# The running sum of a row gather moves into PSUM, and its rows are issued at a closer pace

## The chip, the cores and the metric

The kernel runs on one core of a Trainium2 chip, as one launch. The metric is the device time of that launch in microseconds (us). The core's engines, as the profile names them: PE (matrix products, with PEld for its weight loads), DVE (vector operations), ACT (activations and copies), POOL (some vector operations, and it issues the gathering DMAs), SP (issues the other DMAs). SBUF is the on-chip memory that all of them work in; PSUM is the small memory that PE writes its products to, which this kernel uses as eight banks of 128 x 512 f32.

## The reference

Two small networks in a row, everything in f32, on 256 tokens of width 1024. The first has two layers, each a feed-forward block, a mixer (retention in the first, latent attention in the second) and another feed-forward block. Its result `x` goes into the second network, which has two layers again; each is a mixer and a mixture of 16384 experts per layer, of which every token uses 128. Beside `x` the second network carries 256 context tokens through its first layer; the context does not depend on `x`.

```python
def second_block(x, c, ctx, c_ctx, ...):
    hl, hc = x, ctx
    for i in range(2):
        ml = (silu(c) @ mod_w[i] + mod_b[i])        # six modulation rows each
        mc = (silu(c_ctx) @ mod_w[i] + mod_b[i])
        xl, xc = modulate(rmsnorm(hl), ml), modulate(rmsnorm(hc), mc)
        yl, yc = _even_mixer(xl, xc, ...) if i == 0 else _odd_mixer(xl, xc, ...)
        hl = hl + ml[2] * yl
        hl = hl + ml[5] * _peer_ffn(modulate(rmsnorm(hl), ml), ...)
        if i == 0:                                    # the context ends here
            hc = hc + mc[2] * yc
            hc = hc + mc[5] * _peer_ffn(modulate(rmsnorm(hc), mc), ...)
    return rmsnorm(hl, final_g)

def _peer_ffn(xt, w_q, keys, u, v):                   # per token
    q = (xt @ w_q).reshape(n, 8, 2, 128)
    sv, si = top_k(einsum('nhpd,hpkd->nhpk', q, keys), 16)
    cand = sv[:, :, 0, :, None] + sv[:, :, 1, None, :]
    cs, ci = top_k(cand.reshape(n, 8, -1), 16)        # 8 heads x 16 experts
    eidx = ...                                        # expert = 128 * si0 + si1
    w = softmax(cs) * gelu(einsum('nd,nhkd->nhk', xt, u[eidx]))
    return einsum('nhk,nhkd->nd', w, v[eidx])
```

The experts of the latent tokens are computed densely (all 16384, with the unused gates at zero); those of the context tokens are gathered, row by row.

## The kernel before

**Two streams.** `run_streams` steps two generators. The main stream is the chain from `x` to the output: memory, the feed-forward block ffn00, retention, ffn01, ffn10, latent attention, ffn11, the even mixer, `peer_dense` of layer 0, the odd mixer, `peer_dense` of layer 1. The side stream has the context's work: its even mixer, its route (`ctx_route`: eight groups of scores, and `route_pick`, which ends in the expert numbers `eidx`), and then `gather`. Each `yield` gives a cost, and the stream whose clock (`tm`, `ts`) is behind goes on; the clock also sets the priority by which a list scheduler then orders every engine's instructions. Each engine executes its list strictly in order, so a row that waits holds all rows behind it on its engine.

**Gather.** For each of two tiles of 128 tokens, 128 rows of the table u0 and then 128 of v0: 512 rows, each an indirect DMA issued by POOL (128 x 1024 f32, 512 KB) into one of `GR` = 6 buffers, and one DVE instruction. For u0 that is a dot product with the tokens `pxm` (`dot`, L306), for v0 a multiply-add into the running sum `py` (L1628). Tokens, rows and sum all lie in SBUF. After every second row the stream yields `s.gcost`, 6.5 all along.

**Modulation beside it.** Every third step of the gather also takes a step of `mod1`: seven modulation slots, each of eight 512 KB weight blocks (loaded by POOL's queue) times a narrow `cT`, 32 products and four for the bias, summed in one PSUM bank (L888).

**PSUM banks.** Three kinds: "acc" has four banks (the accumulators of a feed-forward block or of the downs), "w" two (the products of the main stream's weights), "c" two (the context's products, `mod1`, and the second step of several attention and routing stages).

**Products.** Most f32 weights are split into two parts: ACT casts (`wh`, L248), DVE or POOL subtracts (`wl`, L255), and PE multiplies three times (L357 to L359). A feed-forward block is 22 units; one unit is 48 rows of PE for gate and up and 12 for down, with a product `sg` and a subtraction `hlo` on DVE between them. `peer_dense` has 64 ups and 64 downs. The first `AR` ups run before the downs, the others one per down; each down has a cast `Wh` on ACT (L259) and `Wl` on DVE (L260). Of the ups, the first `NU` are multiplied at full f32 (L404, without a split). Between the route and the downs, `spread_gates` builds the gate matrix.

## Time and profile before

| | |
|---|---|
| time, median of 3 runs | 3910.0 us (3907.83 to 3913.4) |
| the profiled execution: its own time | 3902.65 us |
| its span, first to last instruction | 3899.7 us |
| mean granted PE clock | 0.932 of full speed |
| PE busy | 3444.3 us, 88% |
| DVE busy | 2800.3 us, 72% |
| ACT, POOL busy | 1564.8 us, 1507.2 us |
| data moved by DMA | 938.13 MB, mean 241 GB/s |
| gather's rows on DVE (L306, L1628) | 341.8 and 410.0 us |

Stages of the main stream in the trace, from the span's start: ffn00 to about 565 us, retention to 767, ffn01 to about 1000, ffn10 to about 1213, latent attention to 1330, ffn11 to 1590, even mixer to 1845, `peer_dense` 0 to 2838 (its downs from 2158 to 2827), odd mixer to 3020, `peer_dense` 1 to 3888. The gather's first DMA is issued at 567.4 us and its last at 2807.1 us. The busy shares are means over stages: PE is the busiest engine of the whole and of most stages, yet DVE has almost no free time in some.

### The profile page before, as it was taken

To read this page: it belongs to the slowest core of one execution; us is meant where nothing else is said; L and a number is where in the kernel's file an instruction comes from. 1 tells how busy PE (TensorE), PEld (TensorE's weight loads), DVE (VectorE), ACT (ScalarE), POOL (GpSimd) and SP (SyncE) were. 2 spreads that over 40 slices of the span, in tenths; PEclk is the share of its full clock that TensorE was granted. 3 is DMA by queue.
4 is the path that set the end of the run, shared out by engine and by line. 5 is a ranking of instruction groups with operands and counts; after the bars stand their busy time and mean duration, and the time that the engine had idled before them with its cause. 6 is when DMAs were issued, how large, how long until landed. Compare 5 with 4: busy or idle time off the path is not lost.

```text
span 3899.7 us, 55086 instructions
## 1 busy us (share of the span) xinstructions
PE 3444.3 (88%) x20560; PEld 2939.3 (75%) x20560; DVE 2800.3 (72%) x5086; ACT 1564.8 (40%) x2432; POOL 1507.2 (39%) x1014
## 2 busy tenths in 40 slices
PE   5998868799897889788798899999878999999998
PEld 3776867588686678666687788887665889889987
DVE  4456798867777677877798788889976629754444
ACT  3454433334343443433123344444345215444444
POOL 3423325455554245431335477777710000122221
PEclk9999989899898899867899899999989999999999
DMA  7547459878787478753779999999951447876664
GB/s 271 155 146 236 159 163 381 278 278 279 265 294 274 151 252 306 273 175 97 252 272 361 319 324 331 332 333 321 341 154 34 141 156 253 274 238 216 195 192 151
DMA packets 316508, 938.13 MB, mean 241 GB/s; under 512 B 34512, under 2 KB 99504, under 8 KB 312144
## 3 DMA queue, kind: packets, MB, share of 16 engines
q1 hardware_dynamic: 216912, 578.77, 44.4%
q0 software_dynamic: 99328, 355.85, 25.8%
q8 instruction: 161, 2.64, 0.3%
q14 instruction: 107, 0.88, 0.1%
HBM read 894.82 MB, written 39.68 MB: 240 GB/s over the span
## 4 chain that ended last, share of the span: by engine, by line
PE 34%; issue 10%; DVE 9%; POOL 7%; DMA 5%; ACT 2%; POOLq 0%; SPq 0%; DVEq 0%; ACTq 0%
PE ps L357 8%; PE ps L358 8%; PE ps L359 7%; PE ps L404 6%; POOL pg L1600 4%; POOL wl L255 3%; PE ps L313 1%; DMA raw<-in_ffn 1%; DVE py L1628 1%; DVE wl L255 1%; DVE pg L306 1%; PE ps L1661 1%; DMA raw<-in_ut 1%; PE ps L1112 1%; ACT wh L248 1%
## 5 line engine op out<-in xcount | busy, mean ns | idle before, releaser
L248 ACT CAST wh<-raw 128x1024 fp32r<-128x1024 f32 (+3 forms) x925 | 915.6, 992 | 1028.6 <-PE ps L359 674.5
L255 POOL TENSOR_TENSOR wl<-raw,wh 128x1024 fp32r<-128x1024 f32 (+2 forms) x274 | 641.5, 2342 | 1342.4 <-ACT wh L248 1239.2
L255 DVE TENSOR_TENSOR wl<-raw,wh 128x1024 fp32r<-128x1024 f32 (+3 forms) x651 | 799.7, 1233 | 404.5 <-ACT wh L248 403.7
L357 PE MATMUL ps<-xh,wl 128*128 128x256 f32 x2992 | 868.0, 290 | 69.2 <-POOL wl L255 38.9
L358 PE MATMUL ps<-xl,wh 128*128 128x256 f32 x2992 | 857.2, 287 | 0.0
L359 PE MATMUL ps<-xh,wh 128*128 128x256 f32 x2992 | 856.2, 286 | 0.0
L357 PEld LDWEIGHTS ps<-xh,wl 128*128 128x128 f32 x2992 | 582.9, 195 | 101.6 <-POOL wl L255 51.0
L358 PEld LDWEIGHTS ps<-xl,wh 128*128 128x128 f32 x2992 | 583.3, 195 | 5.3 <-issue 0.7
L359 PEld LDWEIGHTS ps<-xh,wh 128*128 128x128 f32 x2992 | 582.4, 195 | 3.5 <-issue 3.2
L1600 POOL DMA_INDIRECT pg<-in_v,eidx x256 | 371.7, 1452 | 395.2 <-DVE py L1628 200.6
L1600 POOL DMA_INDIRECT pg<-in_u,eidx x256 | 370.3, 1447 | 376.4 <-DVE pg L306 277.3
L358 PE MATMUL ps<-wl,Wh 128*128 128x512 f32 x1024 | 408.0, 398 | 26.0 <-POOL wl L255 14.8
L357 PE MATMUL ps<-wh,Wl 128*128 128x512 f32 x1024 | 403.1, 394 | 12.3 <-DVE Wl L260 12.3
L1628 DVE SCALAR_TENSOR_TENSOR py<-pg,pA,py 128x1024 f32<-128x1024 f32 x254 | 410.0, 1614 | 3.4 <-DMA pg<-in_v,eidx 0.3
L359 PE MATMUL ps<-wh,Wh 128*128 128x512 f32 x1024 | 401.6, 392 | 0.0
L404 PE MATMUL ps<-xf,raw 128*128 128x256 f32 x1696 | 382.8, 386 | 2.3 <-ACT xf L332 2.3
L404 PEld LDWEIGHTS ps<-xf,raw 128*128 128x128 f32 x1696 | 325.3, 194 | 47.2 <-ACT xf L332 3.1
L306 DVE SCALAR_TENSOR_TENSOR pg<-pg,pxm 128x1024 f32<-128x1024 f32 x256 | 341.8, 1360 | 11.6 <-DMA pg<-in_u,eidx 11.4
L358 PE MATMUL ps<-wl,xh 128*128 128x512 f32 (+4 forms) x656 | 254.1, 387 | 13.7 <-POOL wl L255 8.4
L358 PEld LDWEIGHTS ps<-wl,Wh 128*128 128x128 f32 x1024 | 194.2, 190 | 81.3 <-POOL wl L255 22.7
L357 PE MATMUL ps<-wh,xl 128*128 128x512 f32 (+4 forms) x656 | 248.3, 386 | 6.6 <-ACT wh L248 2.8
L359 PE MATMUL ps<-wh,xh 128*128 128x512 f32 (+4 forms) x656 | 248.1, 379 | 0.0
(481 smaller groups left out, 4768.7 us busy)
## 6 DMA issues: line engine op xcount, KB each, us to landing
raw<-in_ffn SPq DMA_DIRECT2D x264, 512.0 KB, 5.1
raw<-in_ut SPq DMA_DIRECT2D x256, 512.0 KB, 5.3
raw<-in_v SPq DMA_DIRECT2D x256, 512.0 KB, 4.9
raw<-in_modw POOLq DMA_DIRECT2D x96, 512.0 KB, 6.5
Gd<-Gst SPq DMA_DIRECT2D x32, 1024.0 KB, 7.2
Gq<-Gd SPq DMA_DIRECT2D x30, 1024.0 KB, 8.4
raw<-in_wq SPq DMA_DIRECT2D x32, 512.0 KB, 3.9
raw<-in_evin POOLq DMA_DIRECT2D x24, 512.0 KB, 4.0
```

What stands on the lines that cost most here:

```text
L248: nc.scalar.copy(hi, src)
L255: eng.tensor_tensor(lo, src, hi.bitcast(F32), op=OP.subtract)
L306: return s.nc.vector.scalar_tensor_tensor(a, a, 1.0, b, op0=OP.mult, op1=OP.mult, accum_out=out)
L313: s.nc.tensor.transpose(dst, src, s.ident[:src.shape[0], :src.shape[0]])
L357: mm(out, a[1], b[0], start=start, stop=False)
L358: mm(out, a[0], b[1], start=False, stop=False)
L359: mm(out, a[0], b[0], start=False, stop=stop)
L404: s.nc.tensor.matmul(out, src[:, k * 128:(k + 1) * 128], xf[:, k], start=(k == 0), stop=(k == 7))
L1112: nc.tensor.matmul(po[:, :128], pt[:, k], srcs[k // 2][key][:, k % 2, h * 128:(h + 1) * 128], start=(k == 0), stop=(k == m - 1))
L1600: nc.gpsimd.indirect_dma_start(out=got[i], out_offset=None, in_=d[tab], in_offset=bass.IndirectOffsetOnAxis(ap=eidx[t][:, k:k + 1], axis=0))
L1628: s.pin(nc.vector.scalar_tensor_tensor(y, gt, wk, y, op0=OP.mult, op1=OP.add))
L1661: nc.tensor.matmul(pb[:, t * 128:(t + 1) * 128], M[:, k, :, t0 + t], OJ[:, (t0 + t) // 2, :, t % 2], start=(k == 0), stop=(k == 1))
```

## The change

The sum `py` and the tokens `pxm` move to PSUM: `gather` opens a PSUM pool of its own, `psg`, of two banks, loads the tokens to SBUF (`pxs`) and lets ACT copy them over. A dot or a multiply-add then has one operand in SBUF (the gathered row) and the other in PSUM. The two "c" banks exist no more as such while the gather runs; they are opened for the context's work up to the end of its route (`pss`) and again in the odd mixer (`pso`). What used "c" in between uses other kinds: the attention and mixer stages "w", the route and the gates of `peer_dense` "acc" (its accumulators are taken later), `mod1` "w", that is the two banks of the main stream's weights. So that `mod1` does not hold such a bank over several steps, it ends a partial sum after every two weight blocks, and DVE collects the four of a slot in SBUF (`modo`).

`GC`, the cost of a gather step, is 5.3 instead of 6.5 until the main stream comes to `peer_dense` 0, and 6.5 from there. In layer 0 `AR`, `NU` go from 19 to 18. The condition `cT` is made once, at the start, and not once for each call of `modulation`.

```diff
     def bank(s, kind="w"):
-        return s.psp.tile([128, 512], F32, tag=kind, name=s.nm("ps"), bufs={"acc": 4, "w": 2, "c": 2}[kind])
+        return (s.psc if kind == "c" else s.psp).tile([128, 512], F32, tag=kind, name=s.nm("ps"), bufs=4 if kind == "acc" else 2)
...
-                pb = s.bank("c")
+                if kind == "c":
+                    pb, o = s.bank(kind), bias
+                else:
+                    o = pl.tile([128, 256], F32, name=s.nm("modo"), tag="modo")
                 for k in range(8):
+                    if kind != "c" and k % 2 == 0:
+                        pb = s.bank(kind)
                     fetch(units.index((l, a, k)) + MP)
                     raw = raws.pop((l, a, k))
                     for ps, ns in qs:
-                        nc.tensor.matmul(pb[ps, :256], c[:, k], raw(ns.start, ns.stop), start=(k == 0), stop=False)
-                    if k % 2:
+                        nc.tensor.matmul(pb[ps, :256], c[:, k], raw(ns.start, ns.stop), start=(k % (8 if kind == "c" else 2) == 0),
+                                         stop=(kind != "c" and k in (1, 3, 5)))
+                    if kind != "c" and k == 1:
+                        nc.vector.tensor_copy(o, pb[:, :256])
+                    elif kind != "c" and k in (3, 5):
+                        nc.vector.tensor_tensor(o, o, pb[:, :256], op=OP.add)
...
-        with s.pool("pgg", side) as op:
+        with s.pool("pgg", side) as op, s.psum("psg") as pg:
...
-                xm = op.tile([128, D], F32, tag="pxy", name=s.nm("pxm"))
-                s.dq(xm, xmd[t])
+                xs = op.tile([128, D], F32, tag="pxy", name=s.nm("pxs"))
+                s.dq(xs, xmd[t])
+                xm = pg.tile([128, D], F32, tag="pxy", name=s.nm("pxm"))
+                nc.scalar.copy(xm, xs)
...
-                y = op.tile([128, D], F32, tag="pxy", name=s.nm("py"))
+                y = pg.tile([128, D], F32, tag="pxy", name=s.nm("py"))
...
-        A0N, AR = ((8, 19), (18, 34))[l]
+        A0N, AR = ((8, 18), (18, 34))[l]
...
-            accs = s.acc4()
...
-                yield from s.route_scores(rp, rp, xT, l, "w", "c", xf=xf)
+                yield from s.route_scores(rp, rp, xT, l, "w", "acc", xf=xf)
...
-            yield from s.modulation("right", [(0, 5)] + [(1, a) for a in (1, 0, 2, 4, 3, 5)], MC[2])
+            yield from s.modulation("right", [(0, 5)] + [(1, a) for a in (1, 0, 2, 4, 3, 5)], MC[2], "w")
...
-GC = (6.5, 6.5)
+GC = (5.3, 6.5)
```

**Order, place one.** PE of the kernel before at the end of the context's scores (`keys` times `pq`, L1460); `ps_1311` to `ps_1313` are accumulators of ffn00, whose 16 units were begun by then.

```order
L357 MATMUL ps_1311<-wh_4920,hlo_4756 128x512
L358 MATMUL ps_1311<-wl_4922,hh_4755 128x512
L359 MATMUL ps_1311<-wh_4920,hh_4755 128x512
L357 MATMUL ps_1312<-wh_4920,hlo_4756 128x512
L1460 MATMUL ps_3858<-keys_3789,pq_3856 128x128 x4
L358 MATMUL ps_1312<-wl_4922,hh_4755 128x512
L359 MATMUL ps_1312<-wh_4920,hh_4755 128x512
L357 MATMUL ps_1313<-wh_4920,hlo_4756 128x512
```

ffn00 goes on at once, and the first rows of `mod1` (L888) stand some 410 rows later, in retention. The same place on PE in the changed kernel, where `xh_2885` belongs to the context and `xh_1241` to ffn00:

```order
L362 MATMUL ps_3787<-xl_2886,wh_3836 128x256
L363 MATMUL ps_3787<-xh_2885,wh_3836 128x256
L1487 MATMUL ps_3854<-keys_3785,pq_3852 128x128 x4
L903 MATMUL ps_4574<-raw_4372,cT_288 32x256
L361 MATMUL ps_4592<-xh_1241,wl_4595 128x256
L362 MATMUL ps_4592<-xl_1242,wh_4593 128x256
L363 MATMUL ps_4592<-xh_1241,wh_4593 128x256
```

The first row of `mod1` (L903) now stands directly behind the scores and ahead of ten of ffn00's 22 units of gate and up and eleven of down. Its weights `raw_4372` are issued by POOL, whose list has ten gather DMAs ahead of them (the first and the last two, then the weights):

```order
L1627 DMA pg_4167<-in_u,eidx_2877 128x1024
L1627 DMA pg_4360<-in_u,eidx_2877 128x1024
L1627 DMA pg_4363<-in_u,eidx_2877 128x1024
L197 DMA raw_4372<-in_modw 128x1024
L197 DMA raw_4374<-in_modw 128x1024
```

These need `eidx`, the end of the pick. In the kernel before, the same weights stood behind ten gather DMAs too, but no row of ffn00 stood behind them on PE.

**Place two.** DVE of the kernel before at the end of the pick (`eq`, `cpart`, `eidx`), with rows of ffn00 (`wl`, `sg`, `hlo`) between the pick's, 26 in all:

```order
L1519 TENSOR_TENSOR eq_4138<-io_4112,rd_4134 128x2048
L255 TENSOR_TENSOR wl_5549<-raw_5537,wh_5547 128x1024
L1522 TENSOR_TENSOR eq_4138<-eq_4138,SIf_4136 128x2048
L514 TENSOR_TENSOR sg_5512<-sg_5512,ps_5439 128x256
L1523 TENSOR_REDUCE cpart_4133<-eq_4138 128x128
L260 TENSOR_TENSOR hlo_5516<-sg_5512,hh_5515 128x256
L255 TENSOR_TENSOR wl_5553<-raw_5539,wh_5551 128x1024
```

In the changed kernel the pick has no row of ffn00 in it, twelve dots follow, and the first product of ffn00, `sg_4665`, stands behind the copy of `mod1`'s first partial sum:

```order
L1591 CAST eidx_2878<-cpart_4110 128x128
L310 SCALAR_TENSOR_TENSOR pg_4167,pA_4179<-pg_4167,pxm_4177 128x1024
...
L310 SCALAR_TENSOR_TENSOR pg_4467,pA_4179<-pg_4467,pxm_4177 128x1024
L906 COPY modo_4573<-ps_4574 128x256
L518 TENSOR_TENSOR sg_4665<-sg_4665,ps_4592 128x256
L259 TENSOR_TENSOR wl_4741<-raw_4562,wh_4739 128x1024
```

**Place three.** DVE of the kernel before among the last six downs of `peer_dense` 0 (`Wl` is one per down, `py` is one per gathered row):

```order
L260 TENSOR_TENSOR Wl_25186<-A_24068,Wh_25185 128x512
L255 TENSOR_TENSOR wl_25191<-raw_25180,wh_25189 128x1024
L1628 SCALAR_TENSOR_TENSOR py_21457<-pg_25073,pA_16722,py_21457 128x1024
L1628 SCALAR_TENSOR_TENSOR py_21457<-pg_25076,pA_16722,py_21457 128x1024
L1628 SCALAR_TENSOR_TENSOR py_21457<-pg_25122,pA_16722,py_21457 128x1024
L260 TENSOR_TENSOR Wl_25229<-A_24180,Wh_25228 128x512
```

In the changed kernel the last rows of the sum and its end (`bc`, `px`) stand at the 45th of the 64 downs, and the remaining downs have no gathered row beside them:

```order
L264 TENSOR_TENSOR Wl_24383<-A_22433,Wh_24382 128x512
L1657 SCALAR_TENSOR_TENSOR py_19704<-pg_24147,pA_14995,py_19704 128x1024
L259 TENSOR_TENSOR wl_24278<-raw_24265,wh_24276 128x1024
L1657 SCALAR_TENSOR_TENSOR py_19704<-pg_24150,pA_14995,py_19704 128x1024
L1743 TENSOR_TENSOR A_24255<-A_24255,Gq_25021 128x512
L1663 TENSOR_TENSOR bc_24367<-bc_24367,py_19704 128x1024
```

Counted on DVE's lists, the gathered rows done when the main stream reaches a point are, before and now: end of ffn00 0 and 36, of retention 60 and 70, of ffn01 108 and 126, of ffn10 156 and 179, of latent attention 168 and 202, of ffn11 222 and 267, start of `peer_dense` 0 256 and 314, its first down 330 and 386, its 46th down 459 and 512. PE's rows of `mod1` in retention go from 117 to 16; 29, 60 and about 60 rows now stand inside ffn00, ffn01 and ffn10, where before they stood between the stages.

## Rows read from the trace of the kernel before

**Rows 1.** Windows: length, busy us (instructions) PE, PEld, DVE, ACT, POOL; clock, DMA, GB/s.
```profile
565.00:767.00 202.00, 154.50 (x894) 126.55 (x895) 167.36 (x374) 70.48 (x123) 99.00 (x101) 0.84 0.90 327
2159.00:2712.00 553.00, 522.32 (x3213) 462.51 (x3214) 483.87 (x409) 234.38 (x272) 394.69 (x209) 0.99 0.94 329
2712.00:2827.00 115.00, 96.65 (x389) 72.06 (x387) 114.40 (x82) 41.91 (x48) 88.74 (x52) 0.99 0.93 341
```

**Rows 2.** ACT's timeline: casts Wh, one per down, in both expert layers.
```profile
2158.64 1.14 ACT L259 CAST Wh<-A 128x512 fp32r<-128x512 f32 x2 [3.68 <-DMA Gd<-Gst]
2712.88 0.62 ACT L259 CAST Wh<-A 128x512 fp32r<-128x512 f32 x1 [1.66 <-PE ps L359]
2827.06 0.62 ACT L259 CAST Wh<-A 128x512 fp32r<-128x512 f32 x1 [1.66 <-PE ps L359]
3451.81 0.61 ACT L259 CAST Wh<-A 128x512 fp32r<-128x512 f32 x1
3463.03 0.61 ACT L259 CAST Wh<-A 128x512 fp32r<-128x512 f32 x1
3708.92 0.62 ACT L259 CAST Wh<-A 128x512 fp32r<-128x512 f32 x1 [1.67 <-PE ps L359]
3714.36 0.62 ACT L259 CAST Wh<-A 128x512 fp32r<-128x512 f32 x1 [1.67 <-PE ps L359]
```

**Rows 3.** ACT's timeline: first and last of the route's eight score copies.
```profile
419.57 0.59 ACT L1463 COPY psc<-ps 128x512 f32<-128x512 f32 x1
491.68 0.59 ACT L1463 COPY psc<-ps 128x512 f32<-128x512 f32 x1 [1.30 <-PE ps L1460]
```

**Rows 4.** DVE's timeline there: feed-forward result, first dot, twelfth dot.
```profile
563.62 1.89 DVE L469 SCALAR_TENSOR_TENSOR xn<-ps,bc 128x512 f32<-128x512 f32 x3
576.77 1.23 DVE L306 SCALAR_TENSOR_TENSOR pg<-pg,pxm 128x1024 f32<-128x1024 f32 x1 [4.23 <-DMA pg<-in_u,eidx]
597.90 1.22 DVE L306 SCALAR_TENSOR_TENSOR pg<-pg,pxm 128x1024 f32<-128x1024 f32 x1
```

**Rows 5.** DVE's groups from 498 to 568 us, the feed-forward's: busy us, mean ns, idle.
```profile
L255 DVE TENSOR_TENSOR wl<-raw,wh 128x1024 fp32r<-128x1024 f32 x14 | 16.9, 1214 | 0.9 <-ACT wh L248 0.9
L260 DVE TENSOR_TENSOR hlo<-sg,hh 128x256 fp32r<-128x256 f32 x6 | 3.3, 555 | 0.0
```

**Rows 6.** POOL's timeline at the start of the gather: start, length, instruction.
```profile
567.36 1.02 POOL L1600 DMA_INDIRECT pg<-in_u,eidx  x1 [0.55 <-DVE eidx L1564]
584.74 1.12 POOL L197 DMA_DIRECT2D raw<-in_modw  x2
```

**Rows 7.** Transfers of the page: issues, KB each, us to landing.
```profile
raw<-in_modw POOLq DMA_DIRECT2D x96, 512.0 KB, 6.5
```

**Rows 8.** ACT's timeline in one feed-forward stage: casts 1 and 18.
```profile
1041.64 0.41 ACT L259 CAST hh<-sg 128x256 fp32r<-128x256 f32 x1
...
1200.53 0.41 ACT L259 CAST hh<-sg 128x256 fp32r<-128x256 f32 x1 [3.27 <-DVE sg L514]
```

**Rows 9.** PE's waits: 760 to 1000, 965 to 1225, 1220 to 1340 us; total, times, longest.
```profile
PE ps L888 <- DMA raw<-in_modw: 8.8, 2, 6.9
PE ps L888 <- DMA raw<-in_modw: 10.5, 4, 6.6
PE ps L888 <- DMA raw<-in_modw: 14.1, 6, 5.8
```

**Rows 10.** The costliest groups of the page: busy us, mean ns, idle before.
```profile
L1628 DVE SCALAR_TENSOR_TENSOR py<-pg,pA,py 128x1024 f32<-128x1024 f32 x254 | 410.0, 1614 | 3.4 <-DMA pg<-in_v,eidx 0.3
L306 DVE SCALAR_TENSOR_TENSOR pg<-pg,pxm 128x1024 f32<-128x1024 f32 x256 | 341.8, 1360 | 11.6 <-DMA pg<-in_u,eidx 11.4
```

**Rows 11.** The running sum's instructions: ns min/median/max, first and last start.
```profile
L1628 DVE SCALAR_TENSOR_TENSOR py<-pg,pA,py x254: 1249/1282/3840, 1124.1 to 2819.9; 128x1024 f32<-128x1024 f32 x127
```

**Rows 12.** DVE groups by form: one input in PSUM, then both in SBUF.
```profile
L912 DVE TENSOR_TENSOR fo<-ps,bc 128x512 f32<-128x512 f32 x4 | 2.7, 692 | 4.8 <-PE ps L359 4.6
L913 DVE TENSOR_TENSOR x<-x,fo 128x512 f32<-128x512 f32 x4 | 2.6, 684 | 0.0
```

More of the change, by code (lines that the diff above doesn't have):

```diff
@@ L849, in mla, with condition, modulation @@
             yield from s.out_proj(x, mix, d["wo1"], g3)
-    def modulation(s, side, slots, cost):
+    def condition(s, pl):
+        nc = s.nc
+        c = pl.tile([128, 8, 32], F32, name=s.nm("cT"))
+        nc.vector.memset(c, 0.0)
+        cr = pl.tile([128, 8, 2], F32, name=s.nm("cR"))
+        s.dq(cr, s.d["cvecT"])
+        nc.scalar.activation(c[:, :, 0:2], cr, AF.Silu)
+        one = pl.tile([128, 32], F32, name=s.nm("one"))
+        nc.vector.memset(one, 1.0)
+        s.cond = (c, one)
+    def modulation(s, side, slots, cost, kind="c"):
         nc, d = s.nc, s.d
@@ L892, in modulation @@
                     nc.tensor.matmul(pb[ps, :256], one[ps.start:ps.start + 1], bias[ps.start:ps.start + 1], start=False, stop=True)
[L893 removed]
+                if kind != "c":
+                    nc.vector.tensor_tensor(o, o, pb[:, :256], op=OP.add)
+                    pb = o
                 if a in (1, 4):
[L895 removed]
+                    pg = s.bank(kind)
                     for ps, ns in qs:
@@ L1633, in gather @@
                 s.dq(x, hc[t])
-                nc.vector.tensor_tensor(y, y, g, op=OP.mult)
-                nc.vector.tensor_tensor(x, x, y, op=OP.add)
+                nc.vector.tensor_tensor(g, g, y, op=OP.mult)
+                nc.vector.tensor_tensor(x, x, g, op=OP.add)
                 s.dq(s.hc1[t], x)
@@ L1837, in side @@
         yield from wait("start")
+        pc = ExitStack()
+        s.psc = pc.enter_context(s.psum("pss"))
         with s.pool("pgo", R) as po:
+            s.condition(po)
             with s.pool("sraw", R) as rp:
```

30 lines of the change are left out of this document (16 added, 14 removed).

## The prediction

> **What bounds the kernel now.** I read the windows first, to see which engine fills which stage. In the downs of `peer_dense` 0 PE is busy for 522 of 553 us, DVE for 484, and DMA stands at 0.94; in the last sixteen downs DVE is full (114.4 of 115 us) and PE is not (96.7); in retention neither PE (154.5 of 202) nor DVE (167) is full, and DMA is at 0.90 [rows 1]. So the gather costs time in three ways: it fills DVE at the end of the downs, it fills DMA and DVE in retention, and its modulation makes PE wait between the stages.
>
> The casts of `Wh` say how much it costs in the downs. In `peer_dense` 1, which has no gather beside it, a down with an up takes 3463.03 - 3451.81 = 11.22 us, and a down alone 5.44 us. In `peer_dense` 0 the 47 downs to 2712.88 took 554.2 us; 45 with an up and 2 without would be 45 x 11.22 + 2 x 5.44 = 515.8, so 38 us are lost. The last 16 took 114.2 us and would be 87.0, so 27 us are lost [rows 2].
>
> Then I read the end of ffn00, since the order moves most there. The eight score copies of the context's route run from 419.57 to 491.68, 10.3 us a group [rows 3]; the first gather DMA is issued at 567.36 and the first modulation weights 17.4 us later [rows 6]. ffn00 is over at 563.6, before the first dot [rows 4].
>
> **The change part by part.** All terms are made against the profiled execution's own 3902.65 us; the median of the runs shown is 3910.0, 7.35 us more, and that is added at the end. What one measurement of this kernel can tell from no change is about 0.2%, 8 us.
>
> *The hole in ffn00, +76.* In the new order PE comes to `mod1`'s first product with ten units of gate and up and eleven of down still to do, and that product waits for weights that POOL issues behind ten gather DMAs, which wait for the end of the pick. I date it so. The scores begin two units earlier, since PE has done 12 units and not 14 by then: at 9.35 us a unit (casts 1 and 18 of a feed-forward stage lie 158.9 us apart [rows 8]) that would be 19 us, but the context's own chain ahead of the scores is only partly PE's, so I take 14, thus 406. The groups have no ffn00 unit between them now; of 10.3 us a group, two units in seven groups were 2 x 9.35 / 7 = 2.7, which leaves 7.6; I take 8.5, since DVE's top-k of a group may then set the pace: the last copy at 466. From the last copy to the first gather DMA it was 75.7 us, of which ffn00's subtractions on DVE took 16.9 + 3.3 [rows 5] and its products a little more; without them 54: the first gather at 520. The weights are issued 17.4 us later and land in 6.5 [rows 6, 7]: PE goes on at 544. Ten and a quarter units at 9.35 are 96 us: ffn00 ends at 640 in place of 563.6. The bounds: +55 if the remaining units run at PE's bare pace and the scores begin 19 us earlier, +95 if groups stay at 10 us and `sg`, which stands behind twelve dots and the copy of `modo`, is late as well: the twelfth dot ended 31.7 us after the first gather DMA (597.90 + 1.22 against 567.36 [rows 4, 6]), 8 us behind the weights.
>
> *Retention, -38.* It has 34 gathered rows in place of 60, and 16 products of `mod1` in place of 117. 26 rows are 26 x (1.36 + 0.08) = 37 us of DVE [rows 10] in a stage where DVE is busy for 167 of 202 us, and 26 x 512 KB, 13.6 MB, which at 327 GB/s is 42 us of a nearly full DMA [rows 1]. PE's 154.5 us set the floor: at most -48. At least -10, if the chain of norms and decays sets it.
>
> *Waits between stages, -27.* PE waits for modulation weights by 8.8, 10.5 and 14.1 us around the ends of ffn01, ffn10 and in latent attention [rows 9], 33.4 in all. The products that wait there stand inside the feed-forward blocks now, fetched two ahead. Most of it goes; between -10 and -35.
>
> *Inside the stages, +12.* Counted on DVE's lists, ffn01, ffn10, latent attention, ffn11 and the even mixer take 8, 5, 11, 11 and 13 rows more than before; at 1.44 us these 48 rows are 69 us of DVE, which is busy for about three quarters of those stages, and `mod1` takes one of the main stream's two "w" banks at times. A quarter of it on the path is 17; less a little for rows that no longer stall, 12. Bounds -15 (the sum in PSUM relieves these stages too) and +30.
>
> *The last downs, -27.* The gather is done at the 45th of 64 downs, so the last 16 run at 5.44 us. The cover that DVE took away is given back whole; -20 if DMA, at 0.93 there [rows 1], holds them up by itself.
>
> *The other downs, -24.* The number of rows beside them is nearly the same, 126 for 129. But a multiply-add costs 1614 ns in the mean, a dot 1360 [rows 10], while the fastest multiply-add is 1249, the median 1282 and the slowest 3840 [rows 11]: the mean is made by stalls of a few, next to POOL's own subtractions. With one operand in PSUM I expect most of these to go. What that is worth on the path is bounded by the 38 us that these downs lose [rows 2]; nothing, if DMA at 0.94 bounds them. I take some two thirds, since PE's waits there are for subtractions and not for weights.
>
> [...]
>
> *What an operand in PSUM costs, 0.* The trace has one pair of the same instruction: 692 ns with an input from PSUM, 684 with both in SBUF [rows 12]. That is 8 ns, 4 us of DVE over 512 rows; nothing in before writes PSUM from DVE.
>
> [...]
>
> *The rest, -4.* The pick of `peer_dense` 0 has two rows less, and the odd mixer has the context's result earlier: -6. One up goes from the gates to the downs, where it takes three products for two slower ones, two casts and two subtractions: +2, hidden in what DVE gains. `condition` at the start costs nothing: it runs beside the memory stage's loads. The 23 additions and 7 copies of `modo`, 128 x 256, are 30 x 0.4 us over 1500 us, off the path; the two copies to PSUM are ACT's, which is busy for two fifths.
>
> Sum: 76 - 38 - 27 + 12 - 27 - 24 - 4 = -32. 3902.65 - 32 + 7.35 = **3878**.
>
> **The rivals.**
>
> *The hole is not given back (slower).* ffn00 ends 76 us late, and retention is bound by its own chain of norms, transposes and decays, so that fewer rows there win 10; the waits for weights only move into the feed-forward blocks: -10 and +25; the last downs -20, the others -5, the rest 0. Together +56, or 3966; where only some of these terms fall short the time lies between 3918 and 3966. It decides where retention and the stages up to `peer_dense` 0 give back less than 30 us of the 76. For it speaks that PE stands still for some 75 us in a place where nothing was lost before; against it that retention has both DVE and DMA loaded with just the rows that it loses.
>
> *The stalls were worth more (faster still).* With the sum in PSUM, POOL's subtractions are no longer held up anywhere, the feed-forward blocks gain 15 and the other downs their whole 38; retention -48, waits -35, last downs -31: 76 - 48 - 35 - 15 - 31 - 38 - 4 = -95, or 3815. It needs the feed-forward pace of 9.35 us to fall towards PE's own. The high DMA share of the downs speaks against it.
>
> *Nothing in sum (3902 to 3918).* The hole takes all that the downs, retention and the waits give; for this it is enough that two of the three give half.
>
> *The hole is not there.* If the weights of `mod1` were there before PE comes to them, the +76 would fall away, and the time be near 3800. POOL's list excludes it: ten gather DMAs, all behind `eidx`, stand ahead.
>
> **How the numbers follow.** My forecast, 3825 to 3902, 0.47; the larger gain, below 3825, 0.09; nothing in sum, 0.13; slower, 0.30; the hole absent, 0.01, counted with the larger gain. The time is that of the first. The range leaves out about one in ten below and one in ten above, the upper part of the slower case: 3825 to 3948. The forecast's own range is 3845 to 3902. Faster by over 0.2%: 0.57; within: 0.13; slower: 0.30.
>
> **What the new profile would show.** PE waiting for `raw<-in_modw` once for 60 to 85 us shortly before 550, and ffn00 ending near 640. Retention from there in about 165 us in place of 202. No wait over 5 us for modulation weights after it. `Wh` casts 5.4 us apart in the last sixteen downs, and a mean of the multiply-adds near 1.3 us. I am wrong if ffn00 ends before 600 (another order of arrival at the weights than I read), if retention still takes over 185 us, or if the multiply-add's mean stays above 1.5 us: then two SBUF operands were not what made some of them slow.

## The result and the profile after

The changed kernel takes 3941.22 us (median of 6 runs, 3916.19 to 3945.97) where the kernel before takes 3911.24. The ratio on record, which is not simply the quotient of the two medians, is 1.0069, with a 95% interval of 1.0046 to 1.0091. Ten more runs on another occasion gave 3933.41 us against 3905.66, 1.0067 (1.005 to 1.0084). By the medians it is slower by 28 to 30 us. Its profiled execution is the fastest of the first six, 3916.19 us; the span of this profile is 14.7 us longer than before's.

The page's head, span and busy time of each engine:

```profile
span 3914.4 us, 55149 instructions
PE 3416.5 (87%) x20576; PEld 2944.5 (75%) x20576; DVE 2688.3 (69%) x5107; ACT 1567.4 (40%) x2434; POOL 1362.2 (35%) x1011
```

DVE has 112 us less to do than before, and the kernel is slower all the same. The place where this begins is in PE's timeline, with the wait before a row and its releaser in brackets:

```profile
547.92 1.06 PE L903 MATMUL ps<-raw,cT 128*32 128x256 f32 x2 [65.91 <-DMA raw<-in_modw]
```

PE stands still for 65.9 us in ffn00, for the first weights of `mod1`, and the rows of ffn00 that stand behind this product on its list stand still with it: the next (L361) starts at 548.91 us, though its operands were there, since DVE and POOL make no `wl` between 475.5 and 555.5 us. The same stretch by windows (columns as in [rows 1]):

```profile
480.00:500.00 20.00, 1.33 (x10) 0.97 (x8) 17.40 (x150) 2.45 (x3) 0.00 (x0) 0.65 0.00 0
500.00:520.00 20.00, 0.00 (x0) 0.00 (x0) 19.73 (x59) 1.33 (x2) 0.00 (x0) 0.50 0.07 27
520.00:550.00 30.00, 2.08 (x7) 1.27 (x8) 21.33 (x32) 0.00 (x0) 15.38 (x17) 0.50 0.63 235
550.00:560.00 10.00, 9.46 (x69) 8.67 (x69) 4.19 (x7) 4.05 (x5) 4.34 (x4) 0.79 0.58 224
```

From 500 to 520 us PE has no product at all, DVE works on the context's route and its pick alone, and the granted clock falls from 0.65 to 0.50. When PE goes on, from 550 to 560, the mean is 0.79. POOL's timeline shows why the weights are late. Its list holds the gather's DMAs ahead of them:

```profile
529.15 1.02 POOL L1627 DMA_INDIRECT pg<-in_u,eidx  x1 [54.37 <-DVE eidx L1591]
541.36 1.16 POOL L197 DMA_DIRECT2D raw<-in_modw  x2
```

And DVE's timeline shows the dating of the prediction step by step, from the second `eidx` to the end of ffn00:

```profile
528.91 0.23 DVE L1591 CAST eidx<-cpart 128x128 int32<-128x128 f32 x1
533.61 1.22 DVE L310 SCALAR_TENSOR_TENSOR pg<-pg,pxm 128x1024 f32<-128x1024 f32 x1 [4.48 <-DMA pg<-in_u,eidx]
558.27 0.42 DVE L906 COPY modo<-ps 128x256 f32<-128x256 f32 x1 [5.23 <-PE ps L903]
558.61 0.41 DVE L518 TENSOR_TENSOR sg<-sg,ps 128x256 f32<-128x256 f32 x1
649.25 2.48 DVE L473 SCALAR_TENSOR_TENSOR xn<-ps,bc 128x512 f32<-128x512 f32 x4 [5.51 <-PE ps L363]
```

The first gather DMA is at 529.2 (forecast 520), PE goes on at 547.9 (544), ffn00 ends at 649.25 (640), 85.6 us behind before's 563.62 [rows 4].

What PE waits for between the stages, in the three places that answer to [rows 9]:

```profile
PE ps L317 <- DVE sm L289: 13.8, 1, 13.8
PE ps L317 <- DVE sm L289: 10.6, 1, 10.6
PE ps L317 <- DVE sm L289: 24.6, 1, 24.6
```

No wait there is for modulation weights any more, and yet PE waits 13.8, 10.6 and 24.6 us, for the chain of norms (`sm`), 49.0 in all. In the windows of [rows 9] the kernel before waited for `sm` as well, 1.2, 6.0 and 4.6 us; with the 33.4 for the weights that is 45.2.

The instructions on the gathered rows, minimum, median and maximum in ns, to be read against [rows 11]:

```profile
L310 DVE SCALAR_TENSOR_TENSOR pg<-pg,pxm x256: 1160/1212/1225, 533.6 to 2187.0; 128x1024 f32<-128x1024 f32 x128
L1657 DVE SCALAR_TENSOR_TENSOR py<-pg,pA,py x254: 1270/1281/1291, 1117.5 to 2712.4; 128x1024 f32<-128x1024 f32 x127
L1655 DVE TENSOR_SCALAR py<-pg,pA x2: 1277/1282/1287, 1116.1 to 2201.4; 128x1024 f32<-128x1024 f32 x2
```

The slowest multiply-add takes 1291 ns where it took 3840. Of the downs of `peer_dense` 0, ACT's timeline has these casts of `Wh`, the first and the last two of 64:

```profile
2220.78 1.14 ACT L263 CAST Wh<-A 128x512 fp32r<-128x512 f32 x2 [4.72 <-DMA Gd<-Gst]
2838.34 0.62 ACT L263 CAST Wh<-A 128x512 fp32r<-128x512 f32 x1 [1.67 <-PE ps L363]
2843.78 0.62 ACT L263 CAST Wh<-A 128x512 fp32r<-128x512 f32 x1 [1.66 <-PE ps L363]
```

and these are the windows of retention, of the downs, and of the last downs:

```profile
649.00:832.00 183.00, 148.55 (x822) 126.09 (x822) 149.53 (x338) 71.74 (x124) 58.68 (x59) 0.82 0.70 243
2225.00:2740.00 515.00, 499.79 (x3143) 452.56 (x3142) 412.42 (x337) 227.93 (x263) 314.62 (x190) 0.99 0.95 335
2740.00:2850.00 110.00, 110.00 (x531) 92.98 (x530) 43.77 (x44) 53.02 (x61) 38.35 (x16) 1.00 0.61 192
```

Retention has DMA at 0.70 where it was 0.90 [rows 1], and PE at 148.5 of 183 us. The last downs run at 5.44 us, with PE full and DVE at two fifths. The 64 downs take 623.0 us from the first cast to the last; they took 668.4 [rows 2]. With the 48th cast, at 2751.96 us, the first 47 take 531.2 us (554.2 before) and the last 16 91.8 (114.2). These 91.8 are more than 16 times 5.44, since `AR` is 18 now and one of the 16 still has an up.

The stages of the two kernels and of seven experiments (their numbers in brackets), in us, each from one profiled execution and measured from the first row of one stage's result on DVE to that of the next (`xn<-ps`, `pa<-ps` and `IJ<-ps` in the timelines); the first column is the time from the start of the span. "pick" is the route of `peer_dense` 0 up to `IJ`, "dense 0" the rest of it. A profile can lie off its kernel's median: the changed kernel's lies 17 to 25 us below, that of experiment 1 lies 15 above.

| kernel | ffn00 ends | retention | ffn01 | ffn10 | latent att. | ffn11 | even | pick | dense 0 | odd |
|---|---|---|---|---|---|---|---|---|---|---|
| before | 563.6 | 203.5 | 232.4 | 239.3 | 127.2 | 222.5 | 254.1 | 164.2 | 828.2 | 165.0 |
| changed | 649.2 | 182.6 | 241.6 | 231.8 | 129.4 | 225.0 | 254.1 | 159.5 | 778.1 | 164.6 |
| mod1 held (1) | 565.1 | 223.4 | 243.1 | 235.7 | 123.7 | 227.9 | 249.5 | 159.7 | 783.5 | 169.6 |
| pace undone (2) | 648.3 | 178.3 | 241.1 | 239.8 | 113.2 | 219.0 | 237.6 | 163.2 | 790.3 | 167.3 |
| sum in SBUF (3) | 656.5 | 187.8 | 251.6 | 240.6 | 130.1 | 234.1 | 260.6 | 159.9 | 797.8 | 164.7 |
| before, pace alone (4) | 561.9 | 216.4 | 233.2 | 234.6 | 120.8 | 234.6 | 261.3 | 162.0 | 802.0 | 164.0 |
| held, pace undone (5) | 562.6 | 201.7 | 234.9 | 234.0 | 118.0 | 226.3 | 247.4 | 163.2 | 785.3 | 165.3 |
| held, SBUF, 6.5 (10) | 568.1 | 204.2 | 242.0 | 234.7 | 118.5 | 236.6 | 245.7 | 165.9 | 829.3 | 169.8 |
| held, SBUF, 5.3 (11) | 557.7 | 217.6 | 248.6 | 246.6 | 125.3 | 241.6 | 260.7 | 159.3 | 795.4 | 164.3 |

### The profile page after: what moved, and what is told of

It is laid out like the page before. It is cut to its first block, busy times and chain, and to the rows that moved or that the text cites. A ratio compares the mean times of both kernels' runs of the same rounds, so it can differ in the third digit from the quotient of the medians.

```text
span 3914.4 us, 55149 instructions
## 1 busy us (share of the span) xinstructions
PE 3416.5 (87%) x20576; PEld 2944.5 (75%) x20576; DVE 2688.3 (69%) x5107; ACT 1567.4 (40%) x2434; POOL 1362.2 (35%) x1011
## 4 chain that ended last, share of the span: by engine, by line
PE 56%; DVE 17%; issue 11%; DMA 8%; POOL 5%; ACT 3%; SPq 0%; POOLq 0%; DVEq 0%; ACTq 0%
PE ps L361 14%; PE ps L362 14%; PE ps L363 14%; PE ps L408 6%; POOL pg L1627 2%; DMA raw<-in_ffn 2%; POOL wl L259 2%; PE ps L317 2%; DVE pg L310 2%; DVE wl L259 2%; DMA raw<-in_modw 1%; DVE py L1657 1%; ACT wh L252 1%; DMA pg<-in_u,eidx 1%; DMA Gq<-Gd 1%
## 5 line engine op out<-in xcount | busy, mean ns | idle before, releaser
L259 DVE TENSOR_TENSOR wl<-raw,wh 128x1024 fp32r<-128x1024 f32 (+3 forms) x653 | 777.1, 1193 | 536.9 <-ACT wh L252 534.0
L259 POOL TENSOR_TENSOR wl<-raw,wh 128x1024 fp32r<-128x1024 f32 (+2 forms) x274 | 621.3, 2269 | 1435.3 <-ACT wh L252 1263.3
L361 PE MATMUL ps<-xh,wl 128*128 128x256 f32 x3008 | 873.6, 290 | 64.1 <-DVE wl L259 33.4
L363 PE MATMUL ps<-xh,wh 128*128 128x256 f32 x3008 | 864.6, 287 | 0.0
L361 PEld LDWEIGHTS ps<-xh,wl 128*128 128x128 f32 x3008 | 589.5, 196 | 93.7 <-DVE wl L259 39.3
L363 PEld LDWEIGHTS ps<-xh,wh 128*128 128x128 f32 x3008 | 589.4, 196 | 3.5 <-issue 3.1
L1627 POOL DMA_INDIRECT pg<-in_u,eidx x256 | 297.9, 1164 | 542.0 <-DVE pg L310 325.4
L1627 POOL DMA_INDIRECT pg<-in_v,eidx x256 | 320.6, 1252 | 306.3 <-DVE py L1657 198.3
L361 PE MATMUL ps<-wh,Wl 128*128 128x512 f32 x1024 | 401.2, 392 | 7.9 <-DVE Wl L264 7.9
L363 PE MATMUL ps<-wh,Wh 128*128 128x512 f32 x1024 | 399.6, 390 | 0.0
L408 PE MATMUL ps<-xf,raw 128*128 128x256 f32 x1664 | 368.9, 382 | 2.3 <-ACT xf L336 2.3
L408 PEld LDWEIGHTS ps<-xf,raw 128*128 128x128 f32 x1664 | 317.1, 192 | 45.8 <-ACT xf L336 3.1
L1657 DVE SCALAR_TENSOR_TENSOR py<-pg,pA,py 128x1024 f32<-128x1024 f32 x254 | 325.6, 1282 | 3.1
L310 DVE SCALAR_TENSOR_TENSOR pg<-pg,pxm 128x1024 f32<-128x1024 f32 x256 | 305.2, 1212 | 22.8 <-DMA pg<-in_u,eidx 22.1
L362 PE MATMUL ps<-wl,xh 128*128 128x512 f32 (+4 forms) x656 | 254.3, 388 | 15.5 <-POOL wl L259 10.6
L361 PE MATMUL ps<-wh,xl 128*128 128x512 f32 (+4 forms) x656 | 248.3, 386 | 6.8 <-ACT wh L252 4.6
L363 PE MATMUL ps<-wh,xh 128*128 128x512 f32 (+4 forms) x656 | 249.4, 380 | 0.0
L361 PEld LDWEIGHTS ps<-wh,Wl 128*128 128x128 f32 x1024 | 193.5, 189 | 46.6 <-DVE Wl L264 7.3
```

What stands on the lines that cost most here:

```text
L259: eng.tensor_tensor(lo, src, hi.bitcast(F32), op=OP.subtract)
L310: return s.nc.vector.scalar_tensor_tensor(a, a, 1.0, b, op0=OP.mult, op1=OP.mult, accum_out=out)
L361: mm(out, a[1], b[0], start=start, stop=False)
L362: mm(out, a[0], b[1], start=False, stop=False)
L363: mm(out, a[0], b[0], start=False, stop=stop)
L408: s.nc.tensor.matmul(out, src[:, k * 128:(k + 1) * 128], xf[:, k], start=(k == 0), stop=(k == 7))
```

## The experiments

**1. mod1 held back until ffn00 is done.**

```diff
+        if not s.modgo:
+            return 0
         s.nalong += 1
         if s.nalong % ME:
             return 0
...
                     yield from s.ffn(x, d[f"ffn{l}0"], gain(6 * l + 0), gain(6 * l + 1))
+                    s.modgo = True
```

> The changed kernel, with the steps of mod1 held back until the main stream has left ffn00; all else as changed. Theory 1 (the loss is the 65.9 us for which PE waits for the first modulation weights in ffn00): that wait is gone, ffn00 ends within 10 us of before's 563.6 us, peer_dense 0 keeps its gain of some 50 us, and the time is 3845 to 3875 us, some 1 to 1.7% faster than before. Rival (the hole only moves work: what stood still is done later by a stage that has to wait instead): retention takes over 215 us in place of 203 and the time stays within 10 us of the kernel before, 3900 to 3920 us.

Measured: 3870.16 us (3866.5 to 3885.63), 0.9906 of before (0.9886 to 0.9925). PE's waits from 440 to 600 us, total, times, longest:

```profile
PE ps L317 <- DVE xn L342: 21.2, 2, 19.3
PE ps L361 <- DVE wl L259: 4.9, 5, 2.5
```

The wait for the weights is gone, ffn00 ends at 565.1, `peer_dense` 0 keeps its gain. The 21.2 us are the norm at retention's start, which before shows too (23.0). Retention does pay some of it back, 223.4 us, but the time says that most of the hole was a loss: 63 to 71 us by the two medians of the changed kernel. The two profiles differ by 30.6 us only, since one is the slowest of its four runs and the other the fastest of its six. The same pair at the old pace, experiments 2 and 5, gives 66 us by medians and 58.5 by profiles. That the shared banks put `mod1`'s product at this place is read from the lists: experiments 2 and 3 rule out the pace and the operand, but no run gave `mod1` a bank of its own in the changed kernel.

**2. The pace undone.**

```diff
-GC = (5.3, 6.5)
+GC = (6.5, 6.5)
```

> The changed kernel with a gather step's cost at 6.5 as before, so that only the pace is undone. Theory 1: the hole in ffn00 stays (a wait of 55 to 70 us), since it comes from the shared bank and not from the pace; the gathered rows reach into the last downs again, which loses some 10 to 25 us there: 3945 to 3965 us. Rival (the closer pace makes the hole and burdens the stages before the experts): the wait is below 30 us and the time at or below 3910 us.

Measured: 3897.52 us (3890.61 to 3910.62), 0.9976 of before (0.9958 to 0.9994). Neither expectation, though the rival's time came true: the hole is untouched,

```profile
PE ps L903 <- DMA raw<-in_modw: 66.5, 1, 66.5
```

so it does not come from the pace, as theory 1 has it; but the kernel is 36 to 44 us faster than the changed one, where theory 1 had it slower. The stages say where: latent attention 113.2 for 129.4, the even mixer 237.6 for 254.1, ffn11 219.0 for 225.0, retention 178.3 for 182.6, and in return 12 us lost in dense 0, 8 in ffn10 and 4 in the pick. The windows of latent attention and the even mixer, first of the changed kernel, then of this one:

```profile
1307.00:1437.00 130.00, 88.10 (x457) 75.14 (x458) 91.55 (x232) 57.56 (x145) 41.45 (x34) 0.80 0.50 170
1660.00:1914.00 254.00, 207.70 (x826) 158.44 (x825) 201.61 (x573) 102.52 (x207) 76.64 (x60) 0.73 0.54 190
```

```profile
1307.00:1422.00 115.00, 86.39 (x484) 72.41 (x485) 75.98 (x221) 56.93 (x142) 32.47 (x29) 0.85 0.50 179
1640.00:1877.00 237.00, 194.84 (x825) 148.68 (x824) 193.99 (x510) 100.41 (x206) 56.03 (x46) 0.75 0.49 172
```

In the changed kernel DVE has 15.6 us more to do in latent attention (14 more gathered rows in the trace) and the stage takes 16.2 longer; in the even mixer it is 13 rows and 16.5 us, of which DVE's busy time has 7.6. The wait for the chain of norms (`sm`) at the start of latent attention is 24.6 us there, above, and here

```profile
PE ps L317 <- DVE sm L289: 15.2, 1, 15.2
```

So in latent attention rows that come between the steps of such a chain seem to be paid for whole. In ffn01 and ffn10 the changed kernel has ten rows more and these cost nothing. That this holds of mixers and feed-forward blocks in general is not shown: between before and experiment 4, where the pace alone differs, latent attention has eight rows more and is 6.4 us shorter, and ffn11 has nine more and is 12 longer. What the profiles do bear is the sum. From the end of ffn00 to the end of the even mixer the changed kernel takes 35.7 us longer than this one, for 57 rows more.

**3. The sum in SBUF, all else as changed.** The pool `psg` and the copy to PSUM are taken out; `pxm` and `py` come from the SBUF pool, as before.

> The changed kernel with the tokens and the running sum in SBUF again, banks and pace as changed. If the operand in PSUM is what takes the stalls away: the multiply-add's mean goes from 1282 ns back over 1500, the downs of peer_dense 0 lose 15 to 35 us, and the time is 3950 to 3980 us. Rival (the downs gained by the rows that moved forward, not by the operand): the mean goes back, yet peer_dense 0 stays within 8 us, and the time is that of the changed kernel within 10 us.

Measured: 3988.4 us (3983.59 to 3990.33), 1.0213 of before (1.0195 to 1.0232). The stalls are back:

```profile
L310 DVE SCALAR_TENSOR_TENSOR pg<-pg,pxm x256: 1161/1218/4344, 536.4 to 2229.5; 128x1024 f32<-128x1024 f32 x128
L1655 DVE SCALAR_TENSOR_TENSOR py<-pg,pA,py x254: 1268/1281/3837, 1139.7 to 2777.6; 128x1024 f32<-128x1024 f32 x127
```

The multiply-add's mean is 1607 ns. That is the first expectation, and more than its price: the operand in PSUM is worth 47 to 55 us here. In the profiles dense 0 loses 20 us; the rest is in ffn00, retention, ffn01, ffn10, ffn11 and the even mixer, 5 to 10 us each, for which the prediction's sum had 5 us in all.

**4. The pace alone**, 5.3 for 6.5 in the kernel before.

> The kernel before with the closer pace alone (5.3 for 6.5 up to peer_dense 0), sum in SBUF and banks as before. Theory 1: no hole, ffn00 ends near 565 us; the rows end before the last downs, which win some 20 to 27 us; the rows that moved forward stall in SBUF and cost 10 to 20 us in the feed-forward stages: 3890 to 3905 us. Rival (those stages have no room for rows): at or over 3915 us.

Measured: 3897.11 us (3890.56 to 3909.33), 0.9974 of before (0.9959 to 0.999). As expected: dense 0 wins 26 us, and the stages ahead of it lose 18 of them (the pick ends at 2024.7 us for 2007.0). These are not in the feed-forward blocks alone, as the expectation had it: retention loses 13 us, ffn11 12 and the even mixer 7, and latent attention and ffn10 are shorter.

**5. Both: mod1 held, pace undone.**

> Both edits of the first two experiments together: mod1 held back until ffn00 is done, and a gather step at 6.5 as before. Theory 1a (the closer pace costs the stages between retention and the experts more than it wins in the downs, hole or no hole): latent attention near 113 and the even mixer near 238 us as with the pace undone, no wait over 10 us for modulation weights in ffn00, peer_dense 0 near 790 us: 3825 to 3850 us, faster than the held version by 20 us or more. Rival (the pace cost time only because the hole had set the streams apart): no faster than the held version, 3860 to 3880 us.

Measured: 3831.52 us (3829.75 to 3839.22), 0.9801 of before (0.9774 to 0.9828): theory 1a. It is faster than the kernel before by about 2%, and than the changed kernel by 102 to 110 us. Its rows take what the changed kernel's take (mean ns behind the busy time):

```profile
L1659 DVE SCALAR_TENSOR_TENSOR py<-pg,pA,py 128x1024 f32<-128x1024 f32 x254 | 325.9, 1283 | 8.1 <-DMA pg<-in_v,eidx 3.8 <-issue 0.8 <-DVE Wl L264 0.2
L310 DVE SCALAR_TENSOR_TENSOR pg<-pg,pxm 128x1024 f32<-128x1024 f32 x256 | 304.1, 1214 | 8.8 <-DMA pg<-in_u,eidx 5.8 <-ACT pxm L1645 1.8 <-issue 0.7
```

dense 0 takes 785.3 us at the old pace, with 43 rows in its last 16 downs, against 783.5 at the closer pace (experiment 1), with none. The casts that begin and end these 16 downs here:

```profile
2664.64 0.61 ACT L263 CAST Wh<-A 128x512 fp32r<-128x512 f32 x1
2763.09 0.62 ACT L263 CAST Wh<-A 128x512 fp32r<-128x512 f32 x1 [1.66 <-PE ps L363]
```

They take 98.4 us with the rows and 91.8 without them; with the sum in SBUF it is 118.8 and 91.8 (experiments 10 and 11). So rows in the last downs cost 27 us with the sum in SBUF and 6.6 with it in PSUM. The last downs were slow in the main because the rows stalled, and only to a small part because there were rows.

**6. No weights for mod1**, in the kernel before: the loads and products of the weights are left out, and the modulation rows of this part come from the bias alone.

```diff
+                    if skip:
+                        if k % 2:
+                            yield cost
+                        continue
                     fetch(units.index((l, a, k)) + MP)
```

> The kernel before, where mod1 leaves out its weight loads and weight products (the modulation rows come from the bias alone). The step of the prediction that took the waits for modulation weights as the price (33 us between the stages): ffn01, ffn10 and latent attention together take 25 us or more less than the 599 us of before. Theory 2 (they lie beside the chain of norms, which ends last anyway): at the same places PE waits for DVE's sm or xn instead, 10 to 25 us each, and these three stages together lose no more than 12 us; what else is gained comes from the 28 MB less of DMA in retention.

Measured: 3888.44 us (3880.5 to 3900.22), 0.9957 of before (0.9942 to 0.9972). ffn01, ffn10 and latent attention together take 598.6 us, before 599.0, as theory 2 has it; retention wins 15.6. But the test is not clean. In latent attention PE now waits for the norms, and the stage is 10.5 us shorter all the same:

```profile
PE ps L313 <- DVE xn L338: 16.7, 1, 16.7
PE ps L313 <- DVE sm L276: 11.7, 1, 11.7
```

At the two other places a product of the bias was left standing, and PE waits 15 to 18 us for that; ffn01 is 9.5 us longer. At the end of retention PE's timeline shows what comes behind it:

```profile
769.83 1.08 PE L896 MATMUL ps<-modb,one 1*32 1x256 f32 x8 [15.43 <-DMA modb<-in_modb]
770.83 1.97 PE L313 MATMUL ps<-cst_base,xn 128*128 128x128 f32 x8
775.49 1.94 PE L313 MATMUL ps<-cst_base,xn 128*128 128x128 f32 x8 [2.68 <-DVE xn L338]
```

PE has the bias, does the first token tile's transposes, and then waits for the second tile's `xn`: the chain was not through. So the run supports theory 2 and does not settle it alone; the stronger evidence is the changed kernel itself, where no wait for weights is left, the waits for `sm` stand in their place, and the three stages are no shorter. There the pace and the number of gathered rows differ as well; experiment 10 has both as before.

**7. The changed kernel again.**

> The changed kernel once more, beside the others on one chip. Its six runs went from 3916 to 3946 us while the kernel before kept within 7 us. If the spread comes from the clock after the hole, the longer executions show a lower granted clock in the records, near 0.918 against 0.925, and the time lost stands in the stages that follow the hole; if it comes from the DMA of the gathered rows, the stages with most rows differ and the clock does not. The median is 3930 to 3945 us.

Measured: 3933.41 us (3918.55 to 3948.24), 1.0067 of before (1.005 to 1.0084). In the first six runs the fastest had a clock of 0.925 and the others 0.916 to 0.920, and this profile (3933.21 us) has 0.920, as the first expectation says; among these ten, too, the fastest (3918.55 us) has the highest clock, 0.926. But this profile's 17 us over the first profile lie in small pieces in nearly all stages (ffn01 and dense 0 3.7 each, odd 4.0), and among the five slower runs of the first six a lower clock does not go with a longer time. The median is in the expected span. What makes the spread stays open.

**8. The weights first:** in the changed kernel, one step of `mod1` ahead of the gather's first DMAs.

```diff
+            next(also)
             for i in range(GL):
                 fetch(i)
```

> The changed kernel, with mod1's first two weight loads issued on POOL's queue ahead of the ten gather DMAs instead of behind them; banks, order of the rows and pace as changed. If the hole is the weights' alone: no wait over 15 us in ffn00, which ends near 575 us, and the time is near 3870 us. If the weights are only the last third of it, and ffn00's products on DVE stand behind the pick anyway: PE goes on some 16 us earlier (at the end of the pick, near 531 us instead of 547) and has done one or two units more by then; the wait falls from 66 to 35 to 50 us with DVE as its releaser, ffn00 ends near 622 us, and the time is 15 to 30 us below the changed kernel, 3905 to 3925 us.

Measured: 3931.07 us (3922.73 to 3937.78), 1.0076 of before (1.0049 to 1.0103): no gain over the changed kernel, where 3870 or 3905 to 3925 were expected. POOL's timeline shows that the loads were not free to go even so:

```profile
518.82 0.54 POOL L197 DMA_DIRECT2D raw<-in_modw  x1 [38.53 <-DVE rd L1540]
534.33 0.54 POOL L197 DMA_DIRECT2D raw<-in_modw  x1 [14.97 <-DVE eidx L1591]
```

The first waits for a copy of the pick (`rd`), whose memory it presumably takes over, the second for the end of the pick. PE's wait before the first product falls to

```profile
522.73 1.06 PE L903 MATMUL ps<-raw,cT 128*32 128x256 f32 x2 [35.59 <-DMA raw<-in_modw]
```

at the low end of the expected span and still with the DMA as its releaser. But three more waits for weights follow it in ffn00; total, times, longest:

```profile
PE ps L903 <- DMA raw<-in_modw: 52.8, 4, 35.6
```

And ffn00 ends at 665.7, not at 622: in this order the main stream stands two units further back, so that twelve units of gate and up and not ten stand behind the first product (192 rows of L363 with `xh`, against 160 in the changed kernel's trace). The size of the loss is set by how much of ffn00 the order puts behind `mod1`, as much as by the date of the weights.

**9. mod1 held back to ffn01**, on top of experiment 5, with every second step in place of every third.

> The version that holds mod1 back and undoes the pace, with mod1 held back further, until ffn01 (and stepped every second time in place of every third, so that it is done before the even mixer needs its memory). If the shared banks cost a wait wherever mod1 stands ahead of dependent rows: the wait of 13.9 us for modo in retention is gone, retention takes near 188 us in place of 202, and the time is 3815 to 3825 us. If that wait lies beside the chain of norms like the weights' waits did: retention stays over 196 us and the time within 8 us of 3831 us.

Measured: 3830.71 us (3823.93 to 3840.46), 0.9826 of before (0.9802 to 0.9849), within 1 us of experiment 5. PE's waits in retention, of experiment 5 and of this one:

```profile
PE ps L317 <- DVE xn L342: 20.3, 2, 19.3
PE ps L317 <- DVE modo L906: 13.9, 1, 13.9
```

```profile
PE ps L317 <- DVE xn L342: 20.8, 2, 18.7
PE ps L317 <- DVE rp L594: 5.4, 2, 2.9
PE ps L317 <- DVE mix L780: 5.1, 1, 5.1
PE ps L362 <- DVE wl L259: 4.8, 3, 3.3
```

The wait for `modo` goes and others of 5 us come; the stage is 198.5 for 201.7. Once more a wait for `mod1` lay beside a chain that takes nearly as long.

**10 and 11. Held, with the sum in SBUF, at 6.5 and at 5.3.**

> mod1 held back until ffn00 is done, pace at 6.5, tokens and running sum in SBUF: the held version with the pace undone (3832 us), less the operand in PSUM. It is the kernel before but for the banks and mod1's start. If the operand is the gain of that version: within 15 us of the kernel before, 3890 to 3920 us. If part of the gain comes from the banks or from the later start: 3850 to 3885 us.

Measured: 3904.96 us (3897.12 to 3915.62), 0.9997 of before (0.9979 to 1.0014). The banks, the partial sums on DVE, the moved up, `condition` and the later start of `mod1` come to nothing together; the whole gain of experiment 5, 73 us, is the operand in PSUM. At the closer pace the operand is worth 55 us (experiments 11 and 1). This kernel also is the cleanest test of theory 2. In the three places of [rows 9] PE waits for no weights, but for `sm`:

```profile
PE ps L317 <- DVE sm L289: 14.1, 1, 14.1
PE ps L317 <- DVE sm L289: 16.1, 1, 16.1
PE ps L317 <- DVE sm L289: 16.9, 1, 16.9
```

and ffn01, ffn10 and latent attention take 595.2 us where before took 599.0, at the same pace and with 110 gathered rows for 108: of 33.4 us of waits 3.8 are won.

> The same at the closer pace, 5.3. The closer pace won 10 us in the kernel before and cost 39 us with the sum in PSUM and mod1 held. Theory 3 (it has nothing left to win in the last downs once a row there no longer stalls, and its cost ahead of the experts is much the same in all): with the sum in SBUF it wins its 20 to 30 us in the downs again, and this kernel lies between 10 us below and 15 us above its sister at 6.5. Rival (mod1 in the main stream's banks makes the closer rows dear, wherever the sum lies): 30 to 45 us above its sister.

Measured: 3924.78 us (3910.59 to 3935.12), 1.0047 of before (1.0028 to 1.0066), 20 us above its sister. That lies between the two expectations. The closer pace is worth -11 us with the old banks, +20 with the new ones, `mod1` held and the sum in SBUF, +39 with the sum in PSUM. The stages bear out half of theory 3: dense 0 wins 34 us by the pace in this pair and 2 us in the pair with PSUM. That the pace is dearer by 31 us with the new banks and the held `mod1` is measured; which of the two does it, and by which wait, is not.

## Why the prediction was wrong

By medians, and with one part changed at a time, the way from before to the changed kernel is: the operand in PSUM -73 (experiments 10 to 5), the closer pace +39 (5 to 1), `mod1` in ffn00 +63 to +71 (1 to the changed kernel), all else 0 (before to 10). Together +29 to +37; measured are +28 to +30. These steps form one chain of kernels, so that they add up is no test; and in another order they are of other sizes, since the operand is worth 73 us at the old pace and 47 to 55 at the closer one.

*The hole: the mechanism right, the size 10 us short.* Forecast +76, measured +85.6 by ffn00's end. PE resumed 3.9 us later than dated, and the remaining units took 101 us in place of 96, with 30 gathered rows beside them by the trace.

*What is given back: this step failed.* The sum let retention return 38 and the stages up to the experts 15 more. Retention returned 20.9, and ffn01 to the even mixer took 6.3 more in place of 15 less. These two terms are 38 of the 47 us between the sum, -32, and the profiles' +14.7; the hole is the other 10, nearly. For retention the sum had 26 rows less, at 1.44 us each. The trace has 20 less, 40 for 60, since 30 rows and not 36 had run when ffn00 ended; and the products of `mod1` there fell to about half (83 records on PE for 160), not from 117 to 16. The 20.9 us that these rows and products gave back together are 1.0 us a row. DMA, at 0.70, is no longer nearly full there, DVE is as busy as before (149.5 of 183 us, 167.4 of 202), and PE still stands idle for 34 us. Its longest wait is for the norm:

```profile
PE ps L317 <- DVE xn L342: 16.2, 1, 16.2
```

So part of the stage seems to be a chain that fewer rows shorten little (before, PE's wait there was 23.0 us); what sets the rest of it was not tested.

*Waits between the stages, -27: wrong in kind.* The waits for modulation weights did go, to the letter. They had lain beside the chain of norms, in which PE has nothing to do anyway; PE now waits there for `sm`, 49.0 us in all. The three stages ffn01, ffn10 and latent attention take 602.8 us for 599.0, and 595.2 in experiment 10, where pace and rows are as before: 4 us in place of 27. Most of what is missing in the stages up to the experts is this term. I had read the releaser of a wait as its price without asking what PE would have done had the weights been there.

*Inside the stages, +12: not far off in sum, its parts wrong.* Of this, 17 were for the closer pace and -5 for rows that no longer stall. In ffn01 to the even mixer the pace costs 8.8 us in the kernel before (experiment 4), 19.3 with `mod1` held (1 against 5), 31.4 in the changed kernel (against 2) and 45.4 with the new banks and the sum in SBUF (11 against 10), for 45 to 48 rows more each time; and the operand gives 16.9 back (10 to 5). Each of these is from two single profiles. In which stages the rows cost most differs from pair to pair, and which wait makes them dearer beside the new banks stays open.

*The downs, -27 and -24: the amount nearly right, the cause of the 27 half wrong.* The downs fell by 45.4, the last 16 by 22.4 (the up that moved into them takes 4.8) and the others by 23.0. The 24 were right in amount and cause: the operand alone takes 23.0 off the first 47 downs (experiments 10 and 5), the pace alone nothing (553.8 for 554.2, experiment 4). That one operand in PSUM would end most stalls was my estimate, which no row of the kernel before shows; the changed kernel and experiment 3, which differ in the operand alone, have 1291 and 3837 ns for the slowest multiply-add. The 27 were put down to the rows that finish early. The pace alone does win them (87.0 for 114.2, experiment 4), but the operand alone wins 20 of them with the rows still there (experiment 5), and 6.6 are left for the pace. So the pace was credited with a gain that the operand makes as well, and beside the operand what was left of the pace was mostly its cost.

*The operand: too small.* Forecast -24 in the downs and some 5 elsewhere, measured -73 at the old pace: 44 in dense 0, the rest mostly in feed-forward blocks (7.1 in ffn01, 10.3 in ffn11; experiments 10 and 5). That an operand in PSUM costs a row nothing came true: the dot has a median of 1212 ns with an operand in PSUM, and 1216 in SBUF; the multiply-add 1281 and 1282.

*The median: a part not forecast.* The sum is made against one profiled execution. That of the changed kernel lies 17 to 25 us below its medians, before's only 7, so that 14.7 us of span became 28 us of median; this is the spread of experiment 7.

Of the rivals the slower one came true, in its range of 3918 to 3966 and, in the main, by its mechanism: less than 30 us of the hole were returned ahead of the experts (20.9 less 6.3). Of its parts, waits for weights that move into the feed-forward blocks were not seen. The time lies inside the wide range, 3825 to 3948, which took in part of that rival; the forecast's own, 3845 to 3902, and its direction were missed. The signs named in the prediction read so: one wait of 60 to 85 us, yes (65.9); ffn00's end near 640, 649; retention near 165, no (182.6, short of the 185 that would have said so); no wait over 5 us for weights after it, yes, and worth nothing; last downs 5.4 us apart, yes; multiply-add near 1.3 us, yes.

## What to carry to other kernels

Before a wait is booked as a gain, look for the next thing that the waiting engine needs, and date it: here waits of 33.4 us that lay beside a dependent chain cost 3.8. When two streams share a rotating buffer, the order in which the buffer is handed out can become the order of the work (here this is read from the lists), and one stream's late load holds up the other, here for 65.9 us; give the stream with late data its own buffer, or start it where the other has nothing behind it. Two edits that heal the same loss need not add up (here the pace wins 34 us of dense 0 with the sum in SBUF and 2 with it in PSUM): measure each with the other present.

## What was not expected of the hardware

The stalls of the multiply-adds vanish altogether with one operand in PSUM: the spread of 254 instructions is 1270 to 1291 ns, where it was 1249 to 3840. In the kernel before the slow ones stand beside POOL's subtractions: from 2712 to 2758 us five pairs of multiply-adds take 4.6 us each, every one with a subtraction of 2.55 to 2.62 us beside it, and the other multiply-adds there take 1.27 to 1.33 us. What makes the one slow beside the other is not shown. POOL gains too: its gather DMAs of v0 have a median of 987 ns on the engine, 1466 before. Experiments 5 and 10, which differ in the operand alone, have 976 and 1480 ns, and 1291 and 3835 ns for the slowest multiply-add.

The scaled copy that begins the sum, one operand and the result only, takes 1277 and 1287 ns into PSUM, and took 745 and 754 ns into SBUF in experiment 3. For the multiply-add the place of the sum makes no such difference: its median is 1281 ns in the changed kernel and in experiment 3.
